# Moving one of two opening loads to a second issuing queue, in a kernel that sums rows

## The chip, the cores and the metric

One core of one Trainium2 chip. The time is device microseconds of one execution. The profiles are single executions taken with the hardware profiler. Their span (160.6 us for the kernel before) runs from the first to the last instruction of the kernel; the measured time of an execution is 1.7 to 1.9 us longer than its span. A profiled execution need not be a typical one: the two traces of the kernel before took 162.43 and 162.46 us, more than its median of 162.27, and so a difference of 0.1 or 0.2 us between two traces is not yet one between the kernels.

## The reference

```python
def setup_inputs():
    return {"x": np.random.randn(32, 512, 1024).astype(np.float32)}

def reference(x):
    return np.sum(x, axis=-1).astype(np.float32)
```

67.1 MB are read, 64 KB are written, and each element is added once. There is no reuse, so the kernel is a stream of loads with reductions behind it.

## The kernel before

Each of the 128 partitions holds consecutive rows of 1024 values. Tiles of 16 rows per partition (64 KB in each partition, 8.39 MB in all) go through three buffers, and VectorE reduces a whole tile with one instruction. The last two tiles share their rows with ScalarE, and the last one is loaded in shrinking pieces. The very first tile is loaded in two pieces, one row and then fifteen:

```python
            xt = xpool.tile([P, G * D], F32, tag="xt", name="xt")
            parts = (0, 1, m) if done + c == 0 else (0, m)
            for i, k in zip(parts, parts[1:]):
                nc.sync.dma_start(
                    out=xt[:, i * D : k * D], in_=x_b[:, (c + i) * D : (c + k) * D]
                )
            a = ACT_ROWS if done + c + m == full else 0
            rows_dve(xt, res, 0, m - a, c)
            # ... ScalarE's rows
```

After compilation the kernel edits its own program. This program begins with a barrier of all engines (its last semaphores are at 1.2 us in the trace), and the two first loads wait for nothing, so they are moved ahead of SyncE's arrival at that barrier (its Drain instruction):

```python
    # ... entry: the opening block; body: the block with SyncE's loads
    code = list(body.instructions)
    loads = [i for i in code if i.engine == sp][:EARLY]        # EARLY = 2
    for load in loads:
        assert load.opcode == "DMACopy" and not load.sync_info.on_wait
        code.remove(load)
    body.instructions = code
    code = list(entry.instructions)
    at = next(k for k, i in enumerate(code) if i.engine == sp and i.opcode == "Drain")
    code[at:at] = loads
    entry.instructions = code
```

Of the kernel before, what the change touches and what calls it, by code (L numbers as in the profile page):

```python
# [1 line left out]

# [4 lines left out]

F32 = mybir.dt.float32
ADD = mybir.AluOpType.add
COPY = mybir.ActivationFunctionType.Copy  # L10
X = mybir.AxisListType.X

BLOCKS = (112, 16)
G = 16
ACT_ROWS = 7
CUT = 544
EARLY = 2


@with_exitstack  # L20
def row_sums(
    ctx: ExitStack,
    tc: tile.TileContext,
    x: bass.AP,
    out: bass.AP,
):
    nc = tc.nc
    P = nc.NUM_PARTITIONS

    x_flat = x.flatten_outer_dims()  # L30
    R, D = x_flat.shape
    C = R // P
    assert R % P == 0 and sum(BLOCKS) == C
    out_flat = out.rearrange("a (b c) -> (a b c)", c=1)

    xpool = ctx.enter_context(tc.tile_pool(name="x", bufs=3))
    rpool = ctx.enter_context(tc.tile_pool(name="res", bufs=1))
    part = rpool.tile([P, 1], F32, name="part")
    seen = rpool.tile([P, 1], F32, name="seen")
    pairs = [rpool.tile([P, D // 2], F32, name=f"pairs{i}") for i in range(3)]  # L40

    def rows_dve(xt, res, j, n, c):
        nc.vector.tensor_reduce(  # L43
            out=res[:, c : c + n],
            in_=xt[:, j * D : (j + n) * D].rearrange("p (j d) -> p j d", d=D),
            axis=X,
            op=ADD,
        )

    def sum_act(v, acc):  # L50
        nc.scalar.activation(out=v, in_=v, func=COPY, accum_out=acc)  # L51

    def rows_act(xt, res, j, n, c):
        for i in range(n):
            sum_act(xt[:, (j + i) * D : (j + i + 1) * D], res[:, c + i : c + i + 1])

    def pairs_dve(xt, a, b, first, acc, pairs):
        h = (a + b) // 2
        nc.vector.tensor_tensor_reduce(  # L59
            out=pairs[:, 0 : h - a], in0=xt[:, a:h], in1=xt[:, h:b], scale=1.0, scalar=first,  # L60
            op0=ADD, op1=ADD, accum_out=acc,
        )

    def block(r0, n):
        x_b = x_flat[r0 : r0 + P * n].rearrange("(p c) d -> p (c d)", p=P)
        out_b = out_flat[r0 : r0 + P * n].rearrange("(p c) -> p c", p=P)
        return x_b, out_b, rpool.tile([P, n], F32, name=f"res{r0}")

    full = C - G
    done = 0  # L70
    for b, n in enumerate(BLOCKS):
        x_b, out_b, res = block(done * P, n)
        final = b == len(BLOCKS) - 1
        whole = n - G if final else n
        c = 0
        while c < whole:
            m = min(G, whole - c)
            xt = xpool.tile([P, G * D], F32, tag="xt", name="xt")
            parts = (0, 1, m) if done + c == 0 else (0, m)
            for i, k in zip(parts, parts[1:]):  # L80
                nc.sync.dma_start(
                    out=xt[:, i * D : k * D], in_=x_b[:, (c + i) * D : (c + k) * D]
                )
            a = ACT_ROWS if done + c + m == full else 0
            rows_dve(xt, res, 0, m - a, c)
            rows_act(xt, res, m - a, a, c + m - a)
            c += m
        if not final:
            nc.scalar.dma_start(out=out_b, in_=res)
        done += n  # L90

    xt = xpool.tile([P, G * D], F32, tag="xt", name="xt")
    cuts = [0, 9, 13, 15]
    for i, k in zip(cuts, cuts[1:]):
        nc.sync.dma_start(out=xt[:, i * D : k * D], in_=x_b[:, (c + i) * D : (c + k) * D])  # L95
    last = 15 * D
    for i, k in ((0, CUT), (CUT, D)):
        nc.sync.dma_start(
            out=xt[:, last + i : last + k],
            in_=x_b[:, c * D + last + i : c * D + last + k],  # L100
        )

    for i, k in zip(cuts[:2], cuts[1:3]):
        h = (k - i) // 2
        rows_dve(xt, res, i, h, c + i)
        rows_act(xt, res, i + h, k - i - h, c + i + h)
    pairs_dve(xt, 13 * D, 14 * D, 0.0, res[:, c + 13 : c + 14], pairs[2])
    rows_act(xt, res, 14, 1, c + 14)
    pairs_dve(xt, last, last + CUT, 0.0, part, pairs[0])


    nc.vector.tensor_copy(out=seen, in_=part)  # L112
    pairs_dve(xt, last + CUT, last + D, part, res[:, c + 15 : c + 16], pairs[1])
    nc.sync.dma_start(out=out_b, in_=res)


def kernel(tc: tile.TileContext, x: bass.AP, out: bass.AP):
    row_sums(tc, x, out)
    tc.close()
    tc.compile()  # L120



    sp = mybir.EngineType.SP
    fn = tc.nc.m.functions[0]
    entry, body = None, None
    for blk in fn.blocks:
        ops = [i for i in blk.instructions if i.engine == sp]
        if entry is None:
            entry = blk  # L130
        elif any(i.opcode == "DMACopy" for i in ops):
            body = blk
            break
    code = list(body.instructions)
    loads = [i for i in code if i.engine == sp][:EARLY]
    for load in loads:
        assert load.opcode == "DMACopy" and not load.sync_info.on_wait
        code.remove(load)
    body.instructions = code
    code = list(entry.instructions)  # L140
    at = next(k for k, i in enumerate(code) if i.engine == sp and i.opcode == "Drain")
    code[at:at] = loads
    entry.instructions = code

# [1 line left out]
_INS = ['x']  # L146
_OUTS = [((32, 512), 'float32')]


# [23 lines left out]
```

## Time and profile before

| | kernel before |
|---|---|
| time, median of 3 runs (lowest to highest) | 162.22 us (162.12 to 162.32) |
| span in the profile | 160.6 us |
| bytes over the span | 418 GB/s |
| landing of whole tiles, steady state | every 19.35 us, which is 433 GB/s |
| VectorE for a whole tile | 17.22 us |

First, from the page: the DMA queues (packets, MB, share of the 16 engines' time), the chain of waits that ended last, and the costliest group of instructions (busy time and mean, then the idle time before it and what ended it).

```profile
q1 hardware_dynamic: 2016, 67.12, 97.2%
q10 hardware_dynamic: 144, 0.06, 0.1%
...
DMA 75%; DVE 23%; SPq 0%; issue 0%; DVEq 0%
...
L43 DVE TENSOR_REDUCE res<-xt 128x16 f32<-128x16384 f32 (+3 forms) x9 | 119.8, 13309 | 36.5 <-DMA xt<-in_x_dram 36.5
```

The DMA engines are busy 97% of the span. The chain names VectorE for 23%, but that is not VectorE holding anything up. The chain, in order of time (start, duration, what), shows why:

```profile
1.26 39.99 DMA xt<-in_x_dram
41.25 0.02 issue
41.27 17.23 DVE res L43
58.50 0.02 issue
58.52 40.78 DMA xt<-in_x_dram
```

A load is issued when a reduction frees its buffer, so the chain passes through that reduction. But the load lands 40.78 us after its issue, and most of this is queueing behind the loads in front of it. A chain shows who released whom, and not whether an earlier release would have helped.

Next, the opening of the timeline (start, duration, engine's queue, line), and the issues with their median time from issue to landing:

```profile
0.00 2.25 SPq L81 DMA_DIRECT2D xt<-in_x_dram  x4
...
22.00 17.22 DVE L43 TENSOR_REDUCE res<-xt 128x16 f32<-128x16384 f32 x1 [22.00 <-DMA xt<-in_x_dram]
```

```profile
xt<-in_x_dram SPq DMA_DIRECT2D x1, 7680.0 KB, 21.5
...
xt<-in_x_dram SPq DMA_DIRECT2D x1, 512.0 KB, 3.8
...
xt<-in_x_dram SPq DMA_DIRECT2D x6, 40.8
```

The first line of the timeline merges four issues. In the trace they begin at 0.00 (one row), 0.43 (fifteen rows), 1.26 and 1.64 us. One row (512 KB) lands at 3.8 us, and fifteen (7680 KB) at 0.43 + 21.5 = 21.9 us. Note what did not happen at 3.8 us: no instruction uses the single row. VectorE's reduction needs all sixteen and starts at 22.00 us.

Below the views lie the packet records, one per packet of each DMA engine. The one row is 128 packets of 4 KB, eight per engine; the fifteen rows are 128 packets of 60 KB; a whole tile is 128 packets of 64 KB. In steady state these take 159 ns, 2.267 us and 2.418 us, back to back. The first packets of all are slower:

```
kernel before, the eight 4 KB packets of two engines, put together by matching ends and starts
start us  1.000  1.706  2.057  2.212  2.367  2.523  2.678  2.838   first 60 KB packet at 2.999
took ns     694    354    159    159    159    159    159    159
start us  1.649  2.338  2.493  2.649  2.804  2.959  3.114  3.270   first 60 KB packet at 3.431 (the last engine)
took ns     693    159    159    159    159    159    159    159
```

The records do not name the engine. Where packets of two engines start within a few ns of each other the joining is a guess, as in the first row from its fourth packet on; each packet's start and duration is as recorded.

So there are three stretches: 1.0 us in which nothing moves, about 1 us of slow start, and then full speed to the last load's landing at 157.8 us.

### The profile page before, as it was taken

How to read it: one execution, taken by the hardware profiler on the slowest of the kernel's cores; microseconds unless marked ns; L12 is line 12 of the kernel's file. 1: busy time of each engine (PE TensorE's matmuls, PEld its weight loads, DVE VectorE, ACT ScalarE, POOL GpSimd, SP SyncE). 2: the span in 40 equal slices, each digit the busy share in tenths (PEclk: the TensorE clock that was granted, in tenths of full speed). 3: DMA queues.
4: the chain of work that ended last, by engine and by line, in shares of the span. 5: the costliest groups of instructions: out<-in, count | busy, mean ns of one | idle time of the engine just before them, and what ended most of it. 6: DMA issues, size and time to landing. Idle time of an engine off the chain costs nothing.

```text
span 160.6 us, 119 instructions
## 1 busy us (share of the span) xinstructions
DVE 121.5 (76%) x16; ACT 17.2 (11%) x31; POOL 0.2 (0%) x4
## 2 busy tenths in 40 slices
DVE  0000059997799959999499994999949998697884
ACT  0000000000000000000000000000000000695892
POOL 0000000000000000000000000000000000000000
DMA  9988996996996996996996996996996996998991
GB/s 375 490 367 367 490 522 277 506 522 277 506 522 261 522 522 261 522 522 261 522 506 277 522 506 277 522 506 277 522 506 277 522 490 294 441 431 364 436 390 44
DMA packets 2160, 67.18 MB, mean 418 GB/s; under 512 B 496, under 2 KB 624, under 8 KB 880
## 3 DMA queue, kind: packets, MB, share of 16 engines
q1 hardware_dynamic: 2016, 67.12, 97.2%
q10 hardware_dynamic: 144, 0.06, 0.1%
HBM read 67.11 MB, written 0.07 MB: 418 GB/s over the span
## 4 chain that ended last, share of the span: by engine, by line
DMA 75%; DVE 23%; SPq 0%; issue 0%; DVEq 0%
DMA xt<-in_x_dram 75%; DVE res L43 21%; DVE pairs L59 1%; SPq L95 0%; DVE seen L112 0%; DVE part L59 0%; DVE res L59 0%; DVEq L120 0%
## 5 line engine op out<-in xcount | busy, mean ns | idle before, releaser
L43 DVE TENSOR_REDUCE res<-xt 128x16 f32<-128x16384 f32 (+3 forms) x9 | 119.8, 13309 | 36.5 <-DMA xt<-in_x_dram 36.5
L51 ACT ACT_TABLE_LOAD x1 | 1.3, 1283 | 138.1 <-DMA xt<-in_x_dram 138.1
L51 ACT ACTIVATE xt<-xt 128x1024 f32<-128x1024 f32 x15 | 15.6, 1044 | 2.4 <-DMA xt<-in_x_dram 2.3
L51 ACT ACTIVATION_READ_ACCUMULATOR xt<-xt 128x1 f32 x15 | 2.8, 187 | 0.0
L59 DVE CUSTOM_DVE_ANT_0 pairs<-xt 128x512 f32<-128x512 f32 (+1 forms) x2 | 1.1, 567 | 0.2 <-DMA xt<-in_x_dram 0.2
L59 DVE CUSTOM_DVE_ANT_0 pairs<-xt,part 128x240 f32<-128x240 f32 x1 | 0.5, 468 | 0.0
L112 DVE COPY seen<-part 128x1 f32<-128x1 f32 x1 | 0.2, 153 | 0.0
L59 DVE DVE_READ_ACCUMULATOR2_ANT res<- 128x1 f32 x2 | 0.2, 83 | 0.0
L157 POOL MEMSET const-uint8-127<- 128x1 uint8 x1 | 0.1, 102 | 0.0
L157 POOL MEMSET const-bfloat16-1.0<- 128x1 bf16 x1 | 0.1, 101 | 0.0
L157 POOL MEMSET const-float32-0.0<- 128x1 f32 x1 | 0.1, 99 | 0.2 <-issue 0.2
L157 POOL MEMSET const-float32-1.0<- 128x1 f32 x1 | 0.1, 99 | 0.0
L59 DVE DVE_READ_ACCUMULATOR2_ANT part<- 128x1 f32 x1 | 0.1, 83 | 0.0
## 6 DMA issues: line engine op xcount, KB each, us to landing
xt<-in_x_dram SPq DMA_DIRECT2D x1, 7680.0 KB, 21.5
xt<-in_x_dram SPq DMA_DIRECT2D x1, 4608.0 KB, 32.5
xt<-in_x_dram SPq DMA_DIRECT2D x1, 2048.0 KB, 37.1
xt<-in_x_dram SPq DMA_DIRECT2D x1, 1024.0 KB, 39.1
xt<-in_x_dram SPq DMA_DIRECT2D x1, 512.0 KB, 3.8
xt<-in_x_dram SPq DMA_DIRECT2D x1, 272.0 KB, 39.3
xt<-in_x_dram SPq DMA_DIRECT2D x1, 240.0 KB, 39.4
xt<-in_x_dram SPq DMA_DIRECT2D x6, 40.8
```

Source lines behind the costliest of these rows:

```text
L43: nc.vector.tensor_reduce(out=res[:, c : c + n], in_=xt[:, j * D : (j + n) * D].rearrange("p (j d) -> p j d", d=D), axis=X, op=ADD,)
L51: nc.scalar.activation(out=v, in_=v, func=COPY, accum_out=acc)
L59: nc.vector.tensor_tensor_reduce(out=pairs[:, 0 : h - a], in0=xt[:, a:h], in1=xt[:, h:b], scale=1.0, scalar=first, op0=ADD, op1=ADD, accum ...
L112: nc.vector.tensor_copy(out=seen, in_=part)
L157: nc = _bacc.Bacc("TRN2", target_bir_lowering=False, num_devices=1)
```

## The change

Its intent: SyncE issues the two opening loads one after the other, and the fifteen rows wait for the one row's issue to end (0.38 us; theirs begins at 0.43 us). With the one row on ScalarE's queue both are issued at once, and the barrier, which SyncE reached only after two issues (its Drain begins at 0.90 us), opens sooner.

```diff
-EARLY = 2
 ...
             for i, k in zip(parts, parts[1:]):
-                nc.sync.dma_start(
+                q = nc.scalar if k == 1 else nc.sync
+                q.dma_start(
 ...
+    head, code = list(entry.instructions), list(body.instructions)
+    for e in (mybir.EngineType.SP, mybir.EngineType.Activation):
+        load = next(i for i in code if i.engine == e)
+        assert load.opcode == "DMACopy" and not load.sync_info.on_wait
+        code.remove(load)
+        at = next(k for k, i in enumerate(head) if i.engine == e and i.opcode == "Drain")
+        head.insert(at, load)
+    entry.instructions, body.instructions = head, code
```

## The prediction

> **What bounds the kernel now.** The DMA stream. The chain of waits gives 75% of the 160.6 us span to loads and 23% to VectorE, but a whole-tile reduction takes 17.22 us while the 8.39 MB tiles land 19.35 us apart (completion times in the trace: 21.9, 41.3, 60.6 us), so VectorE idles about 2.1 us before each. 8.39 MB in 19.35 us is 433 GB/s; 67.1 MB at that rate is 154.8 us. The packet records show 16 packets in flight almost always from 1.9 to 150 us. The last input lands at 157.8 us. What is not streaming is about 1.0 us before the first packet, about 1 us of slow start, 0.6 us for smaller packets in the last tile, and 2.8 us of tail.
>
> **What the change does.** Before, SyncE issues the one-row load at 0.00 us (0.38 us of issue) and the fifteen-row load at 0.43 us (0.42 us), drains at 0.90 us and passes the barrier at about 1.2 us. After, ScalarE issues the one-row load beside SyncE's. ScalarE reaches its drain at 0.13 us now, so it should issue between 0.0 and 0.15 us. The barrier should open about 0.4 us earlier. No byte and no compute is added.
>
> **What lies on the critical path.** Almost nothing. The 0.43 us saved is hidden: the engines work off the one-row packets until 2.7 to 3.4 us, and only then start on the fifteen rows. The barrier is off the path too: the third load, issued at 1.26 us, is needed at 21 us. [...]
>
> What can move is the slow start. Eight 4 KB packets per engine take 159 ns each in steady state, 1.27 us. But the first two or three take 240 to 830 ns, so an engine that starts at 1.0 us reaches its first long packet at 2.7 to 3.4 us: 0.4 to 1.1 us lost. The slowest engine's lag of about 0.6 us stays to the end (last landings 157.24 to 157.79 us). After, each engine finds a 60 KB packet (2.27 us) early and should pay the cold latency about once. My estimate: the slowest engine gains 0.2 to 0.5 us, unless the cold period lasts until about 2 us whatever the packets are; then nothing.
>
> Interleaving should cost nothing: where the 448-byte store packets alternate with 16 KB load packets (151 to 155 us), each adds about its own 25 ns. The one-row load will land late, near 18 to 22 us, but the reduction waits for the fifteen rows anyhow.
>
> **Prediction.** 161.95 us, range 161.5 to 162.4; faster by over 2%: 0.01, within 2%: 0.98, slower: 0.01. The expected difference, -0.2%, is near the spread of the runs (162.12 to 162.32).
>
> **What would show it.** ScalarE's load issued by 0.15 us; first packets still at about 1.0 us; the one-row completion moved from 3.8 to about 20 us; first tile complete by 21.4 to 21.8 us (was 21.9); later tiles still 19.35 us apart; tail unchanged; span 160.1 to 160.6 us.
>
> **What would make it wrong.** ScalarE issuing late; [...]a bubble at each alternation of queues (eight per engine); a ragged start that gives one engine more lag. Each would show as a first tile landing after 21.9 us, and add tenths, not per cents.

161.95 us is the 162.22 us measured before, less 0.27 us, which lies within the 0.2 to 0.5 us estimated for the slow start.

## The result

| | before | after |
|---|---|---|
| time, median (lowest to highest), 6 runs each | 162.27 (162.12 to 162.49) | 162.37 (162.29 to 162.39) |
| span in the profile | 160.6 | 160.6 |
| fifteen rows issued, us | 0.43 | 0.00 |
| one row issued, us | 0.00 | 0.12 |
| third load issued (after the barrier), us | 1.26 | 0.93 |
| first packet, us | 1.00 | 1.02 |
| one row complete, us | 3.8 | 22.2 |
| fifteen rows complete, us | 21.9 | 22.0 |
| second tile complete, us | 41.25 | 41.31 |
| last load complete, us | 157.79 | 157.75 |

The ratio of after to before is 1.0006, with a 95% interval of 0.9993 to 1.0019: the same. Here and below a ratio is the mean time of one kernel's fast runs over that of the other's in the same rounds, so it is not quite the ratio of the medians quoted.

The changed kernel's lines, in the order in which those of before were shown. The page:

```profile
q1 hardware_dynamic: 1872, 66.59, 96.4%
q10 hardware_dynamic: 288, 0.58, 0.9%
...
DMA 75%; DVE 23%; SPq 0%; issue 0%; DVEq 0%
...
L42 DVE TENSOR_REDUCE res<-xt 128x16 f32<-128x16384 f32 (+3 forms) x9 | 119.8, 13309 | 36.5 <-DMA xt<-in_x_dram 36.5
```

The chain:

```profile
0.93 40.38 DMA xt<-in_x_dram
41.31 0.02 issue
41.33 17.23 DVE res L42
58.56 0.02 issue
58.58 40.78 DMA xt<-in_x_dram
```

The opening of the timeline:

```profile
0.00 1.85 SPq L81 DMA_DIRECT2D xt<-in_x_dram  x3
0.12 0.38 ACTq L81 DMA_DIRECT2D xt<-in_x_dram  x1
...
22.20 17.22 DVE L42 TENSOR_REDUCE res<-xt 128x16 f32<-128x16384 f32 x1 [22.20 <-DMA xt<-in_x_dram]
```

And the issues with their landings:

```profile
xt<-in_x_dram SPq DMA_DIRECT2D x1, 7680.0 KB, 22.0
...
xt<-in_x_dram ACTq DMA_DIRECT2D x1, 512.0 KB, 22.1
...
xt<-in_x_dram SPq DMA_DIRECT2D x6, 40.8
```

Everything on the issuing side moved as intended. 0.5 MB went from q1 to q10, both loads leave within 0.12 us, and the third load's issue moved from 1.26 to 0.93 us. In the chain, this head start is swallowed by the very next step: that load's wait grew from 39.99 to 40.38 us, and its landing stayed (41.25, now 41.31). The one row now takes 22.1 us instead of 3.8, because its 4 KB packets take turns with SyncE's 60 KB packets on every engine. The packet records of this trace show it: the 4 KB packets start in eight rounds of sixteen, one round every 2.419 us from 3.867 us on, and an engine that ends a 60 KB packet at 4.191 us has a 4 KB packet of the other queue from 4.187 and a 60 KB packet again from 4.342. The turns cost no gap: from the start of a 60 KB packet to the next start it is 2.264 us in both kernels, whichever queue comes next. Nobody was waiting for the one row alone, so its lateness costs nothing either.

The start itself, in the packet records: the sixteen first 60 KB packets started between 1.02 and 2.15 us and took 2.27 to 3.27 us, with a median of 3.04, against 2.267 in steady state.

### The profile page after: what moved, and what is told of

It reads as the page before. It is cut to its first block, busy times and chain, and to the rows that moved or that the text cites. A ratio compares the mean times of both kernels' runs of the same rounds, so it can differ in the third digit from the quotient of the medians.

```text
span 160.6 us, 119 instructions
## 1 busy us (share of the span) xinstructions
DVE 121.5 (76%) x16; ACT 17.2 (11%) x31; POOL 0.2 (0%) x4
## 4 chain that ended last, share of the span: by engine, by line
DMA 75%; DVE 23%; SPq 0%; issue 0%; DVEq 0%
DMA xt<-in_x_dram 75%; DVE res L42 21%; DVE pairs L58 1%; SPq L95 0%; DVE seen L112 0%; DVE part L58 0%; DVEq L120 0%; DVE res L58 0%
## 6 DMA issues: line engine op xcount, KB each, us to landing
xt<-in_x_dram ACTq DMA_DIRECT2D x1, 512.0 KB, 22.1
```

## The experiments

Two measures are used throughout: the time, and the moment when the second tile is complete. The latter tells when the slowest engine got going, since from then on all engines work through equal bytes. It can be checked: in the eight traces of kernels with three buffers and a first tile that is not cut by partitions, the profiled execution took 121.1 to 121.3 us more than its second tile's landing. All kernels gave correct results. The edits are against the changed kernel and in short form; in the runs a list named FIRST holds the loads of the first tile, which go ahead of the barrier unless the text says otherwise. The letters of the theories are those of the expectations, which define them. "Before" beside each had 162.27 or 162.28 us as its median.

### Both loads behind the barrier

```diff
-    for e in (mybir.EngineType.SP, mybir.EngineType.Activation):   # hoists
+    for e in ():
 # and the one row on nc.sync, as in the kernel before
```

> Positive control: both first loads stay on SyncE, behind the barrier, as they would without any hoisting. Theory A (a cold period of about 1 us counted from the first packet): the first packet comes about 0.55 us later than in the kernel before (1.55 us after the first instruction), the second tile lands last at about 41.8 us (41.25 before), and the time is about 0.5 us longer (162.75). Theory B (the DMA engines get up to speed at a fixed moment, about 2 us after the program's start, whatever was issued until then): second tile still at 41.3 us, time within 0.15 us of before.

Measured: 163.04 us, ratio 1.0046 (1.0034 to 1.0059). First packet at 1.72 us (1.00 before), second tile at 42.00 us. The timeline:

```profile
0.73 0.84 SPq L82 DMA_DIRECT2D xt<-in_x_dram  x2
1.62 0.90 SPq L84 DMA_DIRECT2D xt<-in_x_dram  x2
...
22.75 17.22 DVE L44 TENSOR_REDUCE res<-xt 128x16 f32<-128x16384 f32 x1 [22.75 <-DMA xt<-in_x_dram]
```

And from the chain, the wait that ends with the second tile:

```profile
1.62 40.38 DMA xt<-in_x_dram
42.00 0.02 issue
```

The first issue moved by 0.73 us, the first packet by 0.72, the second tile by 0.75 and the time by 0.77 (163.04 less 162.27). (Theory A had expected only 0.5 us, because it put the barrier's delay at 0.55 us.) So in this kernel a delay of the first issue goes into the time one to one, and the measurement can see an effect of this size. Theory B, a fixed moment for full speed, falls. What counts is the *first* issue, and the change leaves it at 0.00 us. In every run here this first issue is SyncE's; that one on ScalarE's queue would do as well was not tried.

### One load of sixteen rows

```diff
-            parts = (0, 1, m) if done + c == 0 else (0, m)
+            parts = (0, m)          # one load, on nc.sync, hoisted
```

> The first tile as one SyncE load of sixteen rows ahead of the barrier, no second early load at all. Theory A (cold period independent of packets and queues): second tile lands last at 41.2 to 41.4 us, time within 0.15 us of before. Theory C (the one-row load on ScalarE's queue is what held the changed kernel back[...]): second tile at 41.0 us or earlier, time 0.2 us or more below before.

Measured: 162.31 us, ratio 1.0003 (0.999 to 1.0015). In its one trace the second tile was complete at 41.00 us, as theory C expected, and the span was 160.4. But that execution, at 162.17 us, was the quickest of its five, and the median does not show the 0.2 us. First packets took 2.83 to 3.29 us against 2.418. So the second early load is worth nothing on either queue, and theory C, that ScalarE's queue held the changed kernel back, falls by the time.

### First 16 partitions, then the other 112

```diff
+FIRST = [('sync', 0, 16, 0, 16 * D), ('sync', 16, 128, 0, 16 * D)]   # queue, partitions, columns
 ...
+            for q, p0, p1, i, k in FIRST:
+                getattr(nc, q).dma_start(out=xt[p0:p1, i:k], in_=x_b[p0:p1, i:k])
```

> SyncE's two early loads are cut by partitions instead of rows: first 16 partitions (one 64 KB packet for each of the 16 engines), then the other 112. Theory A: first packets near 1.0 us, first packet of each engine about 0.6 to 1.0 us longer than the 2.42 us of steady state, second tile last at 41.2 to 41.4 us, time as before within 0.15. Theory D (the slow start is the time it takes to make 128 descriptors; three engines of the changed kernel got their first packet only at 2.0 to 2.15 us): all 16 engines start within about 0.15 us of each other and run at full speed, second tile at 40.9 us or earlier, time about 161.9.

Measured: 184.24 us, ratio 1.1364. Neither theory had expected it. Of the first load each engine had one 64 KB packet, and these took 7.2 to 9.3 us instead of 2.4, about 5 to 7 us too long. The larger part of the 22 us came after that: the 112 packets of the other load took 3.0 to 6.1 us, with a median of 4.7, and the first tile was complete only at 44.06 us.

### Two halves of the partitions, one on each queue

```diff
+FIRST = [('sync', 0, 64, 0, 16 * D), ('scalar', 64, 128, 0, 16 * D)]
```

> Partitions 0 to 63 of the first tile come from SyncE's queue, 64 to 127 from ScalarE's, both ahead of the barrier, 64 descriptors each. Theory A: second tile last at 41.2 to 41.4 us, time as before within 0.15. Theory D (making descriptors is the limit[...]): slow start shorter by about half, 0.4 us, second tile near 40.9 us, time about 161.9.

Measured: 182.39 us, ratio 1.1238. The chain begins:

```profile
0.12 41.98 DMA xt<-in_x_dram
42.10 0.02 issue
42.12 17.22 DVE res L44
```

The first tile took 42.1 us instead of 21.9, and the later ones 19.35 us each as ever: the loss is that one tile's. The packet records show all engines working on SyncE's half until 6.1 to 7.0 us, then all on ScalarE's half, in step, each 64 KB packet taking 4.9 us where 2.418 is normal. In both cuts by partitions the packets took longer than the 2.418 us of a load of all 128: 4.9 us with 64 partitions, which is 2.0 times as long, 7.2 to 9.3 us with 16, which is 3.0 to 3.9 times, and 4.7 us in the median with the other 112. What makes them slow was not shown; it stays open. So these two runs do not decide theory D: a larger cost came in front of the question. One thing can still be read. With one packet per engine in the first load (16 partitions), one engine's first packet still started only at 2.38 us, so ragged starts do not need a load of 128 packets.

### Both kernels once more

> The changed kernel itself once more, for a second trace and five more paired times. If the engines' start-up is ragged by chance, the set of engines that get their first packet late differs from the first trace (there three began at 1.97 to 2.15 us), and the last landing of the second tile moves by 0.1 to 0.3 us from 41.31. If it is fixed by the program, the same three late starters come back within 0.1 us. Time against before: ratio 0.999 to 1.001 under theory A.

> The kernel before once more: ratio 1.000 within 0.001 against itself, which is the noise to hold the others against. Second trace: second tile's last landing within 0.3 us of 41.25; if it differs by as much as the kernels differ from each other (0.25 us between before and one load), those trace differences are chance.

Measured: the changed kernel 162.39 us, ratio 1.0005 (0.9991 to 1.0018); the kernel before 162.28 us, ratio against itself 0.9998 (0.9985 to 1.0011). Second tile complete at 41.31 us (changed) and 41.21 us (before), which repeats the first traces within 0.04 us. The late starters did not come back: where three engines of the first trace started at 1.97 to 2.15 us, only one of the second started after 1.3, at 1.64. So how many engines start late differs from run to run, and yet the slowest landing did not move, where the expectation had tied the one to a shift of 0.1 to 0.3 us in the other.

### Only SyncE's load ahead of the barrier

```diff
-    for e in (mybir.EngineType.SP, mybir.EngineType.Activation):
+    for e in (mybir.EngineType.SP,):
```

> The change with half of it undone: the one-row load stays on ScalarE's queue but behind the barrier, only SyncE's fifteen rows are hoisted. Theory A and a stream that is busy anyway: ScalarE's issue moves from 0.13 to about 0.7 us, its packets still alternate with SyncE's from the second packet on, second tile last at 41.1 to 41.4 us, time within 0.15 us of before. If being ahead of the barrier matters for that load: time at least 0.3 us longer.

Measured: 162.41 us, ratio 1.0006 (0.9994 to 1.0019), second tile at 41.28 us. ScalarE's issue moved from 0.12 to 0.77 us. Its packets alternated later than expected (the one row was complete at 24.4 us, and VectorE began there), and still the time stayed. Half of the change can be undone for nothing.

### The queues exchanged

```diff
+FIRST = [('sync', 0, 128, 0, D), ('scalar', 0, 128, D, 16 * D)]
```

> The two queues exchanged: one row on SyncE ahead of the barrier, fifteen rows on ScalarE ahead of the barrier, 0.12 us after SyncE's. Under A and E which queue carries which load is immaterial: first packets near 1.0 us, second tile last at 41.1 to 41.4 us, ratio to before 0.999 to 1.001. If SyncE's queue is served first or ScalarE's is slower to start, the fifteen rows land 0.3 us or more later than in the changed kernel (21.96 us).

Measured: 162.48 us, ratio 1.0006 (0.9992 to 1.0019). The expectation held for the time but not for the landings: second tile at 41.54 us, and

```profile
xt<-in_x_dram ACTq DMA_DIRECT2D x1, 7680.0 KB, 34.2
...
xt<-in_x_dram SPq DMA_DIRECT2D x1, 512.0 KB, 10.8
```

with the timeline, cut off at 60 us,

```profile
34.30 34.34 DVE L44 TENSOR_REDUCE res<-xt 128x16 f32<-128x16384 f32 x2 [34.30 <-DMA xt<-in_x_dram]
```

and the chain

```profile
0.12 34.16 DMA xt<-in_x_dram
34.28 0.02 issue
34.30 85.73 DVE res L44 x5
```

SyncE's second tile now shares the engines with the fifteen rows on ScalarE's queue, so the first tile is complete at 34.3 us, 12 us later than before. And the time is the same within the noise (the trace is of the slowest of the five, 162.65 us). This is the clearest picture of the slack: VectorE starts 12 us late, works without a pause through five tiles until 120.03 us, and the loads behind it never starve. In this kernel neither the landing of the first tile nor the start of VectorE decides anything; what decides is how soon the engines run at full rate (0.73 us later in the run with both loads behind the barrier, which cost 0.77 us).

### One input buffer: many starts from idle

```diff
-    xpool = ctx.enter_context(tc.tile_pool(name="x", bufs=3))
+    xpool = ctx.enter_context(tc.tile_pool(name="x", bufs=1))
```

> The changed kernel with one input buffer instead of three, much slower on purpose (about 270 us): each tile's load now waits for the reduction of the tile before, so the DMA engines stand idle about 17 us and start afresh seven times, and no other load is issued during the first tile. Theory E (slow start belongs to every start from idle): at each restart the first packet of most engines takes 0.5 us or more longer than 2.42 us. Theory F (slow start only once per execution): at the first tile the first packets take 2.9 to 3.3 us as before, at the restarts 2.42 us plus 0.1 at most. Theory G (the loads issued behind the first one slow it down): even the first tile's first packets take about 2.27 us, since nothing follows.

Measured: 293.55 us (one run, as a measuring kernel; state unknown; about 270 had been expected). The chain shows a start from idle:

```profile
22.08 17.23 DVE res L44
39.31 0.02 issue
39.33 21.82 DMA xt<-in_x_dram
```

A tile costs 21.82 us from an idle start, where it costs 19.35 us in the stream: each start loses about 2.5 us. The packet records show the larger part of that loss:

```
issue at us        39.33   78.41  117.39  156.59  195.71  234.98
first packet after  0.97    0.96    0.95    0.94    0.95    0.95   us
first packets took  3.22    3.19    3.15    3.10    3.15    3.11   us, median of 16 (steady state 2.418)
```

All six restarts look like the first start of the program: about 0.95 us with nothing, then a first packet 0.7 to 0.8 us too long. Theory F (once per execution) falls, and so does theory G (loads issued behind it), since nothing was issued behind these. Theory E stands: each of the six starts of a load from idle was slow.

### Probes on idle engines

As the run before, with a small load or copy ahead of tiles 2 to 7. A copy of the last row sum into the probe's buffer makes it wait for the reduction, and a copy out of it makes the tile's load wait for the probe:

```diff
+PROBES = [('hbm', 128, 16), ('hbm', 128, 1024), ('hbm', 1, 16 * 1024), ('hbm', 16, 16),
+          ('sbuf', 128, 16 * 1024), ('sbuf', 128, 1024)]        # source, partitions, elements
 ...
+                    nc.vector.tensor_copy(out=probe[:, 0:1], in_=res[:, c - 1 : c])
+                    nc.sync.dma_start(out=probe[0:np_, 0:w], in_=src)
+                    nc.vector.tensor_copy(out=xt[0:np_, 0:1], in_=probe[0:np_, 0:1])
                 nc.sync.dma_start(out=xt[:, : m * D], in_=x_b[:, c * D : (c + m) * D])
```

> A measuring kernel, not a candidate: one input buffer as in the run before it, and ahead of tiles 2 to 7 a small extra load or copy on idle DMA engines, each waited for before the tile's own load is issued: 128 x 64 B, 128 x 4 KB, 1 x 64 KB and 16 x 64 B from HBM, then 128 x 64 KB and 128 x 4 KB from another buffer in SBUF. Theory H (the slow start is made at the HBM read side): the two copies inside SBUF run at full rate from their first packet, the HBM loads have first packets 0.3 us or more longer than steady. Theory I (it is made in the engines or queues, at any start): the SBUF copies show the same 0.5 to 1.0 us on the first packets. Theory J (it wears off with recent use): the tile loads issued well under 1 us after a probe has landed start at full rate (first packets 2.42 us plus 0.1), while in the run with one buffer the restarts took 2.9 to 3.4 us; if instead they show the same 2.9 to 3.4 us, a warm-up load cannot help. If descriptors were slow to make, the 16-descriptor probe would be much quicker from issue to landing than the 128-descriptor one of the same row size; expected under A: within 0.2 us of it.

Measured: 343.68 us (one run, state unknown, each probe once). The chain gives each probe's time from issue to landing, and that of the tile's load behind it:

```profile
39.40 1.58 DMA probe<-in_x_dram
...
41.07 0.17 DVE xt L93
41.25 22.01 DMA xt<-in_x_dram
...
80.79 3.68 DMA probe<-in_x_dram
...
123.99 4.59 DMA probe<-in_x_dram
...
168.16 1.48 DMA probe<-in_x_dram
...
281.86 2.90 DMA probe<-spare
...
284.85 0.16 DVE xt L93
285.02 21.68 DMA xt<-in_x_dram
```

- A warm-up does not help. The first probe lands at 40.98 us and the tile's load is issued 0.27 us later; it takes 22.01 us, and its first packets took 3.17 us in the median; behind the five other probes it was 3.07 to 3.13. Theory J falls as it was stated. About 1.6 us pass without a packet between the first probe's last packet and the tile's first, so a shorter gap was not tried.
- Making 128 descriptors, as theory D had it, is not the slow part. 128 x 64 B took 1.58 us and 16 x 64 B took 1.48 us.
- Crowding of the engines is not it either. One 64 KB packet on one engine alone (the third probe) took 3.38 us where 2.418 is normal.
- The source matters. 128 x 4 KB from HBM took 3.68 us; from SBUF it took 2.90 us, though its issue itself took 0.14 us longer. In the packet records the first sixteen 4 KB packets from HBM took 522 ns in the median, against 159 for all; from SBUF they took 167 against 161. The 64 KB copy from SBUF also ran at one pace from its first packet (3.7 to 3.9 us each, median of all 3.78).

So the slow start was seen only with reads of 4 KB and more from HBM (theory H; packets of 64 B took 8 to 11 ns throughout), and not with the copies inside SBUF (theory I falls). What in the path from HBM causes it was not tried. One observation does not fit a simple latency per engine: engines that got their first packet late (at 2.0 us or after in the changed kernel's first trace) ran it at full speed, 2.27 us. It looks as if reads from HBM as a whole come up to rate about 2 us after the first issue; that reading is argued, not shown.

## Why the prediction was right or wrong

**Right: what bounds the kernel, and that the 0.43 us are hidden.** The stream of loads sets the time. The third load's issue came 0.33 us earlier and its wait grew by 0.39 us. So the second queue saved issue time and nothing of the kernel's: ratio 1.0006, and 1.0006 again with the queues exchanged.

**Right: interleaving is free, and the issue times.** The queues' turns leave no gap (2.264 us from start to start in both kernels), ScalarE issued at 0.12 us, first packets came at 1.02 us, the one row landed at 22.2 us (about 20 was named), tiles still land 19.35 us apart, and the tail did not change (span 160.6).

**Wrong: the gain from the slow start.** The step, as it stood: "each engine finds a 60 KB packet (2.27 us) early and should pay the cold latency about once. My estimate: the slowest engine gains 0.2 to 0.5 us". Measured: the second tile was complete at 41.31 us in both traces against 41.25 and 41.21, so the slowest engine gained nothing; averaged over the 16 engines it was even 0.2 us later (41.04 and 41.01 against 40.82 and 40.86). The two slow packets of an engine looked like a price per packet, payable once if the first packet were long. The traces show that a long first packet pays no less. Counted alike, from 1.0 us and against the steady rate, an engine lost 0.5 to 1.2 us with eight short packets (mean 0.75 and 0.79 in the two traces), and 0.6 to 1.2 us with one long packet (mean 0.95 and 0.92). This fits a stretch of time rather than a price per packet, and with it the sentence's own exception, "unless the cold period lasts until about 2 us whatever the packets are; then nothing"; the reading as a stretch is argued, as said above. Hence 162.37 us where 161.95 was named. That this lies inside the range (161.5 to 162.4) is luck and no success of the step: the range reached past the time of before, and the result is at its very edge and on the other side of before.

**Wrong: a mark to watch.** "First tile complete by 21.4 to 21.8 us" was 22.2, and a later landing was to mean a loss. With the queues exchanged the first tile came at 34.3 us at the same time. The first tile's landing says how packets of two queues were mixed, and not how much has been moved; the second tile's landing was the mark to take, as all bytes ahead of it have passed by then.

**Open.** The changed kernel's medians lie 0.1 us above before in every batch (162.37, 162.39), but each interval includes no difference. Put together, the 11 executions of the changed kernel have a mean of 162.38 us and the 20 of before beside them 162.29; the 0.09 us are about two and a half standard errors. So a small loss is likelier than a gain. Whether the 0.2 us of the average engine makes it was not tried.

No version here beats both kernels. The single hoisted load is as fast (1.0003) and simpler. To gain, a version would have to start the first read sooner (first packet at 1.00 us, after the change 1.02) or shorten the tail (about 2.8 us from the last landing to the end of the span, in both), and the change does neither.

## What to carry to other kernels

When all DMA engines are busy from the first packet to the last, count from the first issue: its delay entered the time one to one here (0.73 us late cost 0.77), while later issues, a second queue and the order of landing made no difference above 0.2 us, as the engines never ran dry. Look for the slack before costing a saving: a saved 0.4 us on an issue is worth nothing if its packets then queue 0.4 us longer. And cut a load by columns, not by partitions, when its pieces should run at full rate: cut by columns, the 60 KB packets took 2.267 us here, at the rate of the whole tiles' 64 KB in 2.418 us, while the two cuts by partitions cost 20 and 22 us.
